# Four edits to the order of work: first weight pieces on one queue, splits ahead of casts, RG-LRU gates together, squares in another ring

## The chip, the core and the metric

The kernel runs on one core of one Trainium2 chip. The core has engines that run side by side, each in the order of its own queue: TensorE (PE; its weight loads are shown apart, as PEld), VectorE (DVE), ScalarE (ACT), GpSimd (POOL) and SyncE (SP). The metric is the device time of one execution in microseconds; lower is better. Before the change it is 1039.3 us, the median of three runs from 1038.3 to 1039.59.

## What is computed

A trunk of two layers over 256 tokens of width 2048, in float32. The even layer mixes tokens with an HGRN2 (8 heads of 128) beside a Griffin RG-LRU (8 blocks of 128); the odd layer with a chunkwise mLSTM (8 heads, keys of 128, values of 256). Each is followed by an output projection and a gated embedding. Cut to what the change touches:

```python
def rg_lru(xc, w_r, b_r, w_i, b_i, lam):           # even layer, 8 blocks of 128 features
    r  = sigmoid(einsum('bsnc,ncd->bsnd', xh, w_r) + b_r)
    ig = sigmoid(einsum('bsnc,ncd->bsnd', xh, w_i) + b_i)
    log_a = -8 * r * softplus(-lam)
    a = exp(log_a)
    u = sqrt(-expm1(2 * log_a)) * (ig * xf)
    h = scan(h -> a * h + u)

def mlstm(q, k, v, li, lf):                        # odd layer, per head
    sc  = einsum('bhtd,bhsd->bhts', q, k) * wts    # stabilised exponential weights
    num = (state part) + einsum('bhts,bhse->bhte', sc, v)

pl = rmsnorm(p[i] @ ple_w[i]) * ple_norm[i]        # embedding of width 256, at the very start for i = 0
h  = h + sigmoid(h @ ple_gate_w[i]) * pl
```

## The kernel before

**Products in three terms.** A float32 product is made from two rounded parts of each operand, high and low: high by high, high by low, low by high. For each weight piece `load_weights` (L121) issues a load into a `raw` tile (ring of 5), a cast to the high part `whi` on ScalarE (L132), and the subtraction that gives the low part `wlo` on VectorE (L133); `whi` and `wlo` have rings of 4 tiles of 128 x 1024. The three matmuls of a term group are L193, L194, L195. A projection of 512 columns is made in four quarters of the 2048 input features. A quarter has two tiles of weights and 24 matmuls: 12 for the first 128 tokens, 12 for the other 128, so that the first tile is done with after 18 of them. Results stand in PSUM: pool `pm` (tag `mm`, 3 tiles), `px` (tag `mx`, 3 tiles), `pst` (tag `st`, 2 tiles).

**Order of the work.** The code is written as a chain of projections on TensorE, with the rest of the layer in coroutines ("lanes"). In the middle of each quarter `pump` (L75) moves every lane one `yield` further, so TensorE's part of a lane is placed behind the matmul issued last. A planner orders each engine's queue by priority: an instruction's place in the program, less the offset of `tc.high_priority(offset=...)` around it. The weight casts and subtractions carry offset 400 (L131), the reading of the second branch's gate projection 450 (L876), some other readings of PSUM 100. Tiles of one tag share a ring of slots; a new tile waits for the last reader of the slot's old content.

**The start.** The first work is the embedding's projection. `load_head` (L268) loads the first two feature blocks of `p` and the first weight tile in four pieces of 256 columns each, through SP's queue (`sy`) and ScalarE's (`s`), and splits them at offset 900 (L280 to L286). `embed` (L289) runs the matmuls (L316): first those that need only the first half of the features, then those that need pieces three and four. Loads of everything after go through SP's queue in program order.

**RG-LRU** (`rg_lru`, L778), one coroutine for each half of the 8 blocks: split of inputs and weights; gates of blocks 0 and 1 (`j = 0`: matmuls L151 to L153 through `mm3`, sigmoids L801, in `st` tiles), a `yield`, gates of blocks 2 and 3, a `yield`; then tanh and exponential (L808, L809), squares (L814, in two tiles of tag `th`, a ring of 2) and L815, which reads them; square root; scan. The gate projection of the second branch (L873 to L886) reads its PSUM with a tanh into a tile of the same tag `th` (L879), a scaled copy (L880) and a product (L881). Tag `hn` is another ring, of 3 tiles, for scaled projections and rearranged features. The attention of the even layer (L610 on) uses `mx` tiles at the same stage.

**mLSTM.** Queries and keys come from a projection, a convolution (L979) and a SiLU (L982, L983). `mix(j)` (L1051) handles heads 2j and 2j+1: it spreads the running maxima (L231), builds the weights, splits queries and keys into high and low parts (L1074 on ScalarE, L1075 on VectorE), forms the scores (L1081, L1082), multiplies (L1083), splits again, and multiplies by the values (L1101). Meanwhile the values are projected in four groups (L1126): ScalarE writes the scaled high part `vt` from PSUM (L1133), VectorE the low part `vl` (L1134); both tiles of `pm` that a group holds come free with that.

Of the kernel before, what the change touches and what calls it, by code (L numbers as in the profile page):

```python
# [11 lines left out]
F32 = mybir.dt.float32  # L12
# [3 lines left out]
AF = mybir.ActivationFunctionType  # L16
ALU = mybir.AluOpType
PSUM = bass.MemoryType.PSUM

P = 128  # L20
# [23 lines left out]
def trunk(ctx: ExitStack, tc: tile.TileContext, a, out):  # L44
    nc = tc.nc
    v, s, gp, te, sy = nc.vector, nc.scalar, nc.gpsimd, nc.tensor, nc.sync
# [5 lines left out]
    tp = ctx.enter_context(tc.tile_pool(name="tp", bufs=2))  # L52
    bp = ctx.enter_context(tc.tile_pool(name="bp", bufs=4))
    pm = ctx.enter_context(tc.tile_pool(name="pm", bufs=3, space=PSUM))
    px = ctx.enter_context(tc.tile_pool(name="px", bufs=3, space=PSUM))
    pst = ctx.enter_context(tc.tile_pool(name="pst", bufs=2, space=PSUM))
# [211 lines left out]
    def load_head(src):  # L268
        praw = tp.tile([P, 512], F32, name="praw", tag="hn", bufs=3)
        raw = wp.tile([P, 1024], F32, name="raw", tag="raw", bufs=5)  # L270
        hi, lo = (wp.tile([P, 1024], F32R, name=n, tag=n) for n in ("whi", "wlo"))
        ph, pl, both = act_pair()

        def piece(x, n):
            return x[:, n * T:(n + 1) * T]

        for q, dst, of, n in ((sy, praw, a["pT"][0], 0), (s, raw, src, 0), (sy, praw, a["pT"][0], 1), (s, raw, src, 1),
                              (sy, raw, src, 2), (sy, raw, src, 3)):
            q.dma_start(out=piece(dst, n), in_=piece(of, n))
        with tc.high_priority(offset=900):  # L280
            for n in range(4):
                if n < 2:
                    v.tensor_copy(ph[:, n], piece(praw, n))
                    v.tensor_tensor(out=pl[:, n], in0=piece(praw, n), in1=ph[:, n].bitcast(F32), op=ALU.subtract)
                s.copy(piece(hi, n), piece(raw, n))
                v.tensor_tensor(out=piece(lo, n), in0=piece(raw, n), in1=piece(hi, n).bitcast(F32), op=ALU.subtract)  # L286
        return (hi, lo), (ph, pl, both)
# [175 lines left out]
    norm = {}  # L463
# [48 lines left out]
    def gate_tok(w, j, act, u):  # L512
# [7 lines left out]
    mx, e0, e1, lb, omb, sp, ez, z2, pol, sp8, spm8 = (small(8, n) for n in (  # L520
        "mx", "e0", "e1", "lb", "omb", "sp", "ez", "z2", "pol", "sp8", "spm8"))
# [44 lines left out]
    if True:  # L566
# [211 lines left out]
        def rg_lru(r):  # L778
            while r not in xcs:
                yield  # L780
            xc = xcs[r]
            bw = wp.tile([P, 2, 512], F32, name="bw", tag="raw", bufs=5)
            sy.dma_start(out=bw, in_=a["bw"][r])
            av = m0.tile([P, 1024], F32, name="av", tag="f")
            tt = m0.tile([P, 1024], F32, name="tt", tag="k")
            it = m0.tile([P, 1024], F32, name="it", tag="it", bufs=1)
            bh, bl = (hp.tile([P, 2, 512], F32R, name=n, tag="h") for n in ("bh", "bl"))
            s.copy(bh, bw)
            v.tensor_tensor(out=bl, in0=bw, in1=bh.bitcast(F32), op=ALU.subtract)
            xs = [split_act(xc[:, j * 512:(j + 1) * 512], "xc") for j in range(2)]  # L790
            yield
            for j in range(2):
                for w, (dst, bias) in enumerate(((av, "bbr"), (it, "bbi"))):
                    ps = pst.tile([P, 512], F32, name="st", tag="st")
                    for i in range(2):
                        c = 2 * j + i
                        mm3(ps[:, i * T:(i + 1) * T], bh[:, w, c * P:(c + 1) * P], bl[:, w, c * P:(c + 1) * P], xs[j], i,
                            True, True)
                    for i in range(2):
                        c = 2 * j + i  # L800
                        gate = s.activation(dst[:, c * T:(c + 1) * T], ps[:, i * T:(i + 1) * T], AF.Sigmoid,  # L801
                                            bias=pc(bias, 4 * r + c)).ins
                yield
            for c in range(4):
                b = 4 * r + c
                cc = slice(c * T, (c + 1) * T)
                with tc.issue_after(gate):
                    s.activation(tt[:, cc], av[:, cc], AF.Tanh, scale=sp8[:, b:b + 1])  # L808
                    s.activation(av[:, cc], av[:, cc], AF.Exp, scale=spm8[:, b:b + 1])  # L809
            v.tensor_tensor(out=it, in0=it, in1=xc, op=ALU.mult)  # L810
            for j in range(2):
                sq = tp.tile([P, 512], F32, name="sq", tag="th")
                jj = slice(j * 512, (j + 1) * 512)
                s.activation(sq, av[:, jj], AF.Square)  # L814
                v.scalar_tensor_tensor(tt[:, jj], sq, 1.0, tt[:, jj], op0=ALU.add, op1=ALU.mult)  # L815
            yield
            s.activation(tt, tt, AF.Sqrt, scale=0.25)
            v.tensor_tensor(out=it, in0=it, in1=tt, op=ALU.mult)
            yield
            v.memset(av.rearrange("p (c t) -> p c t", t=T)[:, :, 0:1], 0.0)  # L820
            v.tensor_tensor_scan(tt, av, it, 0.0, op0=ALU.mult, op1=ALU.add)
            res["h", r] = tt
# [50 lines left out]
        for g in range(2):  # L873
            ps = project_tok(ew, 6 + g, acth)
# [81 lines left out]
    with tc.tile_pool(name="m1", bufs=2) as m1:  # L956
        qk = {}
# [93 lines left out]
        def mix(j):  # L1051
# [17 lines left out]
                yield  # L1069
            qhl = room2("qhl").rearrange("p (s i t) -> p s i t", s=2, i=2)  # L1070
            khl = tp.tile([P, 512], F32R, name="khl", tag="th").rearrange("p (s i t) -> p s i t", s=2, i=2)
            for hl, src in ((qhl, qk[j].rearrange("p (i t) -> p i t", i=2)),
                            (khl, qk[4 + j].rearrange("p (i t) -> p i t", i=2)[:, :, 0:P])):
                s.copy(hl[:, 0], src)  # L1074
                v.tensor_tensor(out=hl[:, 1], in0=src, in1=hl[:, 0].bitcast(F32), op=ALU.subtract)  # L1075
            yield
            for i in range(2):
                q, k = qk[j][:, i * T:(i + 1) * T], qk[4 + j][:, i * T:(i + 1) * T]
# [13 lines left out]
            vh, vl = vts[j]  # L1092
# [33 lines left out]
        for j in range(4):  # L1126
            psv = project_tok(a["ov"], j, acth)
            vt = m1.tile([P, 2, 2, VW], F32R, name="vt", tag="vt", bufs=6)
            gp.memset(vt.bitcast(F32)[:, :, :, 256:VW], 1.0)
            vl = ap.tile([P, 1024], F32R, name="vl", tag="ahl").rearrange("p (h i e) -> p h i e", h=2, i=2)  # L1130
            for hf in range(2):
                src = psv[hf].rearrange("p (i e) -> p i e", i=2)
                s.activation(vt[:, hf, :, 0:256], src, AF.Copy, scale=norm["rt"][:, hf:hf + 1])  # L1133
                v.scalar_tensor_tensor(vl[:, hf], src, norm["rt"][:, hf:hf + 1], vt[:, hf, :, 0:256].bitcast(F32),  # L1134
                                       op0=ALU.mult, op1=ALU.subtract)
            vts.append((vt, vl))
            if j == 0:
                drain("qk0", "qk2")
                for c in range(4):
                    start("mix", mix(c))  # L1140
                start("mix", mix_norm())
# [259 lines left out]
```

## Time and profile before

| what | value |
|---|---|
| median of 3 runs | 1039.3 us (1038.3 to 1039.59) |
| profiled execution, its own time | 1037.71 us |
| its span, first to last instruction | 1035.9 us |
| granted TensorE clock | 0.998 |
| moved by DMA | 234.79 MB, mean 227 GB/s |
| VectorE, weight subtractions L133 | 357, 431.2 us together |
| ScalarE, weight casts L132 | 357, 372.7 us together |

How to read it: times within the execution are microseconds from the start of the span. In the list of waits a row is "who waited <- for whom", with the total, the number of times and the longest. In a timeline a row has the start, the duration, the engine, the line, the operation, the tile written <- the tiles read, the shapes and the count; brackets give the idle time before it and what ended it. Matmuls overlap, so a matmul's duration is longer than the distance to the next one's start.

### The profile page before, as it was taken

To read this page: it belongs to the slowest core of one execution; us is meant where nothing else is said; L and a number is where in the kernel's file an instruction comes from. 1 tells how busy PE (TensorE), PEld (TensorE's weight loads), DVE (VectorE), ACT (ScalarE), POOL (GpSimd) and SP (SyncE) were. 2 spreads that over 40 slices of the span, in tenths; PEclk is the share of its full clock that TensorE was granted. 3 is DMA by queue.
4 is the path that set the end of the run, shared out by engine and by line. 5 is a ranking of instruction groups with operands and counts; after the bars stand their busy time and mean duration, and the time that the engine had idled before them with its cause. 6 is when DMAs were issued, how large, how long until landed. Compare 5 with 4: busy or idle time off the path is not lost.

```text
span 1035.9 us, 14422 instructions
## 1 busy us (share of the span) xinstructions
PE 1025.0 (99%) x5230; PEld 851.1 (82%) x5230; DVE 739.9 (71%) x1130; ACT 599.6 (58%) x863; POOL 89.7 (9%) x169
## 2 busy tenths in 40 slices
PE   9999999999999999999999999999999999999996
PEld 7888888888888888888888888888888888888886
DVE  7858878969686776767569986755457777666684
ACT  7775555577874444565557865644445557344562
POOL 0111101011111121111021000000001111111000
PEclk9999999999999999999999999999999999999999
DMA  9987746567779888687597655455566778787552
GB/s 341 336 240 241 228 152 216 183 197 233 239 239 303 273 246 271 215 269 233 193 280 239 213 171 173 157 182 190 194 200 224 250 255 288 216 278 238 204 184 82
DMA packets 67752, 234.79 MB, mean 227 GB/s; under 512 B 8801, under 2 KB 10081, under 8 KB 67681
## 3 DMA queue, kind: packets, MB, share of 16 engines
q1 hardware_dynamic: 55728, 196.64, 57.5%
q0 software_dynamic: 11520, 36.71, 12.2%
q8 instruction: 41, 0.67, 0.3%
q10 hardware_dynamic: 432, 0.52, 0.2%
q14 instruction: 31, 0.25, 0.1%
HBM read 216.02 MB, written 17.83 MB: 226 GB/s over the span
## 4 chain that ended last, share of the span: by engine, by line
PE 96%; DVE 2%; ACT 1%; issue 1%; DMA 0%; SPq 0%; ACTq 0%; DVEq 0%
PE mm L193 26%; PE mm L195 26%; PE mm L194 26%; PE mx L195 4%; PE mx L193 4%; PE mx L194 3%; PE mm L316 2%; PE nu L1101 1%; DVE wlo L133 1%; PE mm L1233 1%; PE mm L1232 1%; PE mm L1231 1%; PE mx L626 0%; DVE qk L979 0%; DMA raw<-in_pw_dram 0%
## 5 line engine op out<-in xcount | busy, mean ns | idle before, releaser
L133 DVE TENSOR_TENSOR wlo<-raw,whi 128x1024 fp32r<-128x1024 f32 (+1 forms) x357 | 431.2, 1215 | 213.9 <-ACT whi L132 201.7
L132 ACT CAST whi<-raw 128x1024 fp32r<-128x1024 f32 (+1 forms) x357 | 372.7, 1048 | 315.7 <-PE mm L195 248.8
L193 PE MATMUL mm<-whi,ahl 128*128 128x512 f32 x1216 | 474.9, 391 | 0.1
L194 PE MATMUL mm<-wlo,ahl 128*128 128x512 f32 x1216 | 473.4, 389 | 0.0
L195 PE MATMUL mm<-whi,ahl 128*128 128x512 f32 x1216 | 473.0, 389 | 0.0
L193 PEld LDWEIGHTS mm<-whi,ahl 128*128 128x128 f32 x1216 | 228.3, 188 | 48.4 <-issue 0.8
L195 PEld LDWEIGHTS mm<-whi,ahl 128*128 128x128 f32 x1216 | 228.3, 188 | 47.9
L194 PEld LDWEIGHTS mm<-wlo,ahl 128*128 128x128 f32 x1216 | 228.3, 188 | 46.9 <-DVE wlo L133 0.3
L193 PE MATMUL mx<-whi,ahl 128*128 128x512 f32 x160 | 62.2, 389 | 0.0
L194 PE MATMUL mx<-wlo,ahl 128*128 128x512 f32 x160 | 62.2, 389 | 0.0
L195 PE MATMUL mx<-whi,ahl 128*128 128x512 f32 x160 | 62.2, 389 | 0.0
L194 PEld LDWEIGHTS mx<-wlo,ahl 128*128 128x128 f32 x160 | 30.0, 188 | 6.3
L195 PEld LDWEIGHTS mx<-whi,ahl 128*128 128x128 f32 x160 | 30.0, 188 | 6.2
L193 PEld LDWEIGHTS mx<-whi,ahl 128*128 128x128 f32 x160 | 30.1, 188 | 6.2
L477 POOL DMA_DIRECT2D ducn<-w x4 | 2.2, 559 | 214.4 <-DVE w L490 214.4
L979 DVE SCALAR_TENSOR_TENSOR qk<-xr,prm,qk 128x255 f32<-128x255 f32 (+2 forms) x48 | 20.5, 471 | 0.1
L147 DVE TENSOR_TENSOR ahl<-xr,ahl 128x512 fp32r<-128x512 f32 x24 | 16.3, 686 | 4.1 <-ACT ahl L146 4.0
L316 PE MATMUL mm<-whi,ahl 128*128 128x512 f32 x56 | 17.4, 389 | 0.0
L146 ACT CAST ahl<-xr 128x512 fp32r<-128x512 f32 x24 | 14.7, 612 | 4.2 <-DVE xr L831 4.1
L361 DVE STREAM_TRANSPOSE w<-hq 128x512 f32<-128x512 f32 x24 | 16.7, 703 | 0.2
L379 DVE TENSOR_TENSOR ahl<-r,ahl 128x128 fp32r<-128x128 f32 x64 | 13.9, 280 | 2.8 <-ACT ahl L377 2.8
L377 ACT CAST ahl<-r 128x256 fp32r<-128x256 f32 x32 | 10.6, 402 | 5.7 <-DMA r<-dfe 5.6
(330 smaller groups left out, 824.4 us busy)
## 6 DMA issues: line engine op xcount, KB each, us to landing
raw<-in_ew_dram SPq DMA_DIRECT2D x64, 512.0 KB, 5.5
raw<-in_g_dram SPq DMA_DIRECT2D x64, 512.0 KB, 5.1
raw<-in_eo_dram SPq DMA_DIRECT2D x32, 512.0 KB, 5.9
raw<-in_oqk_dram SPq DMA_DIRECT2D x32, 512.0 KB, 4.8
raw<-in_ov_dram SPq DMA_DIRECT2D x32, 512.0 KB, 4.1
raw<-in_oog_dram SPq DMA_DIRECT2D x32, 512.0 KB, 3.7
raw<-in_oz_dram SPq DMA_DIRECT2D x32, 512.0 KB, 4.2
raw<-in_oo_dram SPq DMA_DIRECT2D x32, 512.0 KB, 5.2
```

Of the source, the lines that this page charges most:

```text
L132: last["act"] = s.copy(h, r).ins
L133: last["dve"] = v.tensor_tensor(out=l, in0=r, in1=h.bitcast(F32), op=ALU.subtract).ins
L146: (v.tensor_copy if name == "p0" else s.copy)(hi, src)
L147: v.tensor_tensor(out=lo, in0=src, in1=hi.bitcast(F32), op=ALU.subtract)
L193: te.matmul(ps[hf], xh, wh, start=(k == 0), stop=False)
L194: te.matmul(ps[hf], xh, wl, start=False, stop=False)
L195: last["pe"] = te.matmul(ps[hf], xl, wh, start=False, stop=(k == KT - 1)).ins
L316: last["pe"] = te.matmul(ps[hf][:, o:o + w_], tokens(pact[x], k, hf), (hi, lo)[y][:, k * 512 + o:k * 512 + o + w_], start=(n == mine[0]), ...
L361: v.transpose(w5[:, hf], h[:, hf].rearrange("p (c j q) -> p c j q", c=4, j=4))
L377: s.copy(hk, src)
L379: v.tensor_tensor(out=lk[:, hf], in0=src[:, hf], in1=hk[:, hf].bitcast(F32), op=ALU.subtract)
L979: v.scalar_tensor_tensor(dst[:, sh:T], pi[:, 0:T - sh], pc("ccw", k * 16 + n), dst[:, sh:T], op0=ALU.mult, op1=ALU.add)
```

## The change

Four edits. (1) In `load_head` pieces three and four of the first weight tile are issued on ScalarE's queue, as pieces one and two are. (2) In `rg_lru` the gates of both pairs of blocks are computed in one step of the coroutine, the second pair in `mx` tiles, and two `yield`s follow. (3) The squares take tiles of the ring `hn` instead of `th`. (4) The splits of queries and keys, and the reading of the values from PSUM with their split, carry offset 450.

```diff
         for q, dst, of, n in ((sy, praw, a["pT"][0], 0), (s, raw, src, 0), (sy, praw, a["pT"][0], 1), (s, raw, src, 1),
-                              (sy, raw, src, 2), (sy, raw, src, 3)):
+                              (s, raw, src, 2), (s, raw, src, 3)):
             q.dma_start(out=piece(dst, n), in_=piece(of, n))
...
             for j in range(2):
                 for w, (dst, bias) in enumerate(((av, "bbr"), (it, "bbi"))):
-                    ps = pst.tile([P, 512], F32, name="st", tag="st")
+                    pool, tag = ((pst, "st"), (px, "mx"))[j]
+                    ps = pool.tile([P, 512], F32, name="rg", tag=tag)
...
-                yield
+            yield
+            yield
             for c in range(4):
...
-                sq = tp.tile([P, 512], F32, name="sq", tag="th")
+                sq = tp.tile([P, 512], F32, name="sq", tag="hn", bufs=3)
...
-            for hl, src in ((qhl, qk[j].rearrange("p (i t) -> p i t", i=2)),
-                            (khl, qk[4 + j].rearrange("p (i t) -> p i t", i=2)[:, :, 0:P])):
-                s.copy(hl[:, 0], src)
-                v.tensor_tensor(out=hl[:, 1], in0=src, in1=hl[:, 0].bitcast(F32), op=ALU.subtract)
+            with tc.high_priority(offset=450):
+                for hl, src in ((qhl, qk[j].rearrange("p (i t) -> p i t", i=2)),
+                                (khl, qk[4 + j].rearrange("p (i t) -> p i t", i=2)[:, :, 0:P])):
+                    s.copy(hl[:, 0], src)
+                    v.tensor_tensor(out=hl[:, 1], in0=src, in1=hl[:, 0].bitcast(F32), op=ALU.subtract)
...
-            for hf in range(2):
-                src = psv[hf].rearrange("p (i e) -> p i e", i=2)
-                s.activation(vt[:, hf, :, 0:256], src, AF.Copy, scale=norm["rt"][:, hf:hf + 1])
-                v.scalar_tensor_tensor(vl[:, hf], src, norm["rt"][:, hf:hf + 1], vt[:, hf, :, 0:256].bitcast(F32),
-                                       op0=ALU.mult, op1=ALU.subtract)
+            with tc.high_priority(offset=450):
+                for hf in range(2):
+                    src = psv[hf].rearrange("p (i e) -> p i e", i=2)
+                    s.activation(vt[:, hf, :, 0:256], src, AF.Copy, scale=norm["rt"][:, hf:hf + 1])
+                    v.scalar_tensor_tensor(vl[:, hf], src, norm["rt"][:, hf:hf + 1], vt[:, hf, :, 0:256].bitcast(F32),
+                                           op0=ALU.mult, op1=ALU.subtract)
```

## The prediction

> **What bounds the kernel now.** I read the page first, then the list of who waited for whom, cut down to TensorE and its weight loads, and then the timeline at the few places which that list names.
>
> ```profile
> span 1035.9 us, 14422 instructions
> ...
> PE 1025.0 (99%) x5230; PEld 851.1 (82%) x5230; DVE 739.9 (71%) x1130; ACT 599.6 (58%) x863; POOL 89.7 (9%) x169
> ```
>
> TensorE is busy for 1025.0 of 1035.9 us. The edits remove no matmul, so they can only win back time in which TensorE stands still. The waits of TensorE and of its weight loads:
>
> ```profile
> PE mx L316 <- ACT whi L285: 1.1, 1, 1.1
> ...
> PE mx L1081 <- DVE khl L1075: 0.5, 1, 0.5
> ...
> PEld mm L193 <- ACT u L880: 0.4, 1, 0.4
> ...
> PEld mm L193 <- PE mx L231: 0.3, 1, 0.3
> ```
>
> Columns: who waited, for whom, us in total, times, longest. There are four short places: the start (L316), the score products (L1081), and two places where a projection (L193) cannot start on its next PSUM tile. Each edit touches one of them. These rows count idle time from the modelled end of a matmul, so below I size each place by the distance between matmul starts.
>
> **Part 1, the first weight pieces (L277).** The chain of waits and ScalarE's timeline in the first microseconds:
>
> ```profile
> 2.12 4.40 DMA raw<-in_pw_dram
> 6.55 0.41 ACT whi L285
> ...
> 7.00 2.11 PE mx L316 x8
> ```
>
> ```profile
> 0.74 0.89 ACTq L279 DMA_DIRECT2D raw<-in_pw_dram  x2
> 1.66 1.28 ACT L285 ACT_TABLE_LOAD   x1 [1.66 <-PEq L1392]
> 3.90 0.40 ACT L285 CAST whi<-raw 128x256 fp32r<-128x256 f32 x1 [0.95 <-DMA raw<-in_pw_dram]
> ...
> 7.60 1.27 ACT L132 CAST whi<-raw 128x512 fp32r<-128x512 f32 x2 [0.65 <-DMA raw<-in_pw_dram]
> ```
>
> The fourth piece is issued on SP at 2.12, lands 4.40 us later and is cast at 6.55; only then can the products with the second half of the features begin (7.00). The edit puts pieces three and four behind the first two on ScalarE's queue. Two issues there take 0.89 us, so the third starts at about 0.74 + 0.89 = 1.63 and the fourth at 2.08: the same moment as now. Nothing is won at the issue itself. ScalarE pays two more issues, 0.89 us, and its table load slides from 1.66 to about 2.55, ending at 3.83: still before the first piece is cast at 3.90, so it is covered, with 0.07 us to spare. SP is free 0.9 us sooner, and all its later loads go out that much earlier: the second half's pieces, the next block, the parameters, the first activations.
>
> So the question is when the fourth piece lands once it no longer stands in SP's line. The first 10 us of the transfers (issues with median us to landing; GB/s in 40 slices of 0.25 us):
>
> ```profile
> GB/s 1 0 0 0 0 0 0 135 205 246 213 279 373 369 373 279 238 205 209 148 188 238 246 270 246 279 270 295 270 279 295 311 295 311 336 360 377 303 367 308
> ...
> raw<-in_pw_dram SPq DMA_DIRECT2D x4, 256.0 KB, 5.2
> ...
> raw<-in_pw_dram ACTq DMA_DIRECT2D x2, 128.0 KB, 3.2
> ```
>
> Best end: it lands as fast as ScalarE's pieces do now, 3.2 us after issue, at 5.3; the wait of 1.1 us goes. Worst end: it shares the engines with SP's 256 KB pieces, which are now issued at 1.66 and 2.12, and takes their 5.2 us: 7.3, which is 0.8 us later than now. Bytes say something between: from 1.75 to 6.5 us the slices average about 249 GB/s, 1.18 MB, and the six first pieces with two 256 KB ones are 1.31 MB, which would be done by about 7.0. So -1.1 to +0.8; I take 0, since the row nearest to it is the piece itself, issued at the same moment with 4.40.
>
> [...]
>
> [...]
>
> ```profile
> 580.23 1.05 ACT L132 CAST whi<-raw 128x1024 fp32r<-128x1024 f32 x1 [0.78 <-PE mm L195]
> 581.30 1.28 ACT L982 ACT_TABLE_LOAD   x1
> 582.59 0.63 ACT L982 ACTIVATE th<-qk 128x512 f32<-128x512 f32 x1
> ```
>
> The cast ends at 581.28, the load runs from 581.30 to 582.58 and the next activation starts at 582.59. I go by these rows.
>
> **Part 2, RG-LRU: gates in one group, squares in another ring (L792 to L815).** The same 24 x 2 gate matmuls and 16 sigmoids run; those of the second pair of blocks move up by one step of the coroutine, and two `yield`s keep the exponentials where they were. Their PSUM comes from the three `mx` tiles. The attention uses these too, but one at a time until its read-out, a step later; I cost this at nothing, and if the cover were gone it is a wait of one evacuation, the 0.69 us of the row at 282.26 below. The gain lies at the first gate projection of the second branch. TensorE and ScalarE there:
>
> ```profile
> 282.97 0.39 PE L195 MATMUL mm<-whi,ahl 128*128 128x512 f32 x1
> 283.20 0.88 PE L193 MATMUL mm<-whi,ahl 128*128 128x512 f32 x2
> 283.92 0.39 PE L194 MATMUL mm<-wlo,ahl 128*128 128x512 f32 x1
> ```
>
> ```profile
> 270.41 0.84 ACT L801 ACTIVATE av<-st,prm 128x256 f32<-128x256 f32 x2 [1.74 <-PE st L153]
> ...
> 282.26 0.69 ACT L879 ACTIVATE th<-mm,rth 128x512 f32<-128x512 f32 x1 [0.84 <-DVE tt L815]
> 282.85 0.68 ACT L880 ACTIVATE u<-mm,rcr 128x512 f32<-128x512 f32 x1
> ```
>
> The columns are start, duration and, in brackets, the idle time before. A matmul normally follows the last by 0.23 us (282.97 to 283.20). From 283.20 two of them take 0.72 us to the next start instead of 0.46: 0.26 us lost, because the PSUM tile is only free once L880 has read it at 283.53. L880 is late because the tanh before it stood idle 0.84 us for L815: its `th` slot was still held by a square. With the squares in `hn` that wait goes and L880 ends about 0.8 us earlier, before 283.20. The gates moved away from 270.41 free another 2 x 0.84 us of ScalarE ahead of it. **Gain 0.26 us**; bounds 0 and 0.26.
>
> **Part 3, values split ahead of the casts (L1131).** TensorE, ScalarE and VectorE at the first group of values:
>
> ```profile
> 589.55 0.39 PE L231 MATMUL mx<-s,identr 128*128 128x256 f32 x2
> 590.04 0.47 PE L193 MATMUL mm<-whi,ahl 128*128 128x512 f32 x1
> 590.35 0.39 PE L194 MATMUL mm<-wlo,ahl 128*128 128x512 f32 x1
> ```
>
> ```profile
> 584.63 0.69 ACT L1133 ACTIVATE vt<-mm,rcr 128x512 fp32r<-128x512 f32 x1
> ...
> 588.03 0.68 ACT L1133 ACTIVATE vt<-mm,rcr 128x512 fp32r<-128x512 f32 x1
> ```
>
> ```profile
> 589.14 0.75 DVE L1134 SCALAR_TENSOR_TENSOR vl<-mm,rcr,vt 128x512 fp32r<-128x512 f32 x1
> ```
>
> ScalarE has read the first half by 585.32, but VectorE reads it last only from 589.14 to 589.89; the next projection's second tile is the same bank, and it starts at 590.04. Two 256-column matmuls and the restart take 0.80 us from 589.55 to 590.35 instead of about 0.46: 0.34 us lost. Moved ahead of the weight casts, the subtraction follows ScalarE by the time VectorE is next free, more than 3 us early. **Gain 0.34 us**; bounds 0 and 0.34.
>
> **Part 4, queries and keys split ahead of the casts (L1074).** The first and the second head pair on TensorE, then VectorE and ScalarE at the first:
>
> ```profile
> 606.48 0.52 PE L1081 MATMUL mx<-qhl,khl 128*128 128x256 f32 x3
> ...
> 608.36 0.47 PE L193 MATMUL mm<-whi,ahl 128*128 128x512 f32 x1
> ```
>
> ```profile
> 627.23 0.52 PE L1081 MATMUL mx<-qhl,khl 128*128 128x256 f32 x3
> ...
> 628.30 0.48 PE L193 MATMUL mm<-whi,ahl 128*128 128x512 f32 x1
> ```
>
> ```profile
> 603.85 0.69 DVE L983 SCALAR_TENSOR_TENSOR qk<-th,qk 128x512 f32<-128x512 f32 x1 [0.76 <-ACT th L982]
> 604.79 2.36 DVE L133 TENSOR_TENSOR wlo<-raw,whi 128x1024 fp32r<-128x1024 f32 x2 [0.25 <-ACT whi L132]
> 607.07 0.42 DVE L1075 TENSOR_TENSOR khl<-qk,khl 128x256 fp32r<-128x256 f32 x1
> ```
>
> ```profile
> 605.61 0.40 ACT L1074 CAST khl<-qk 128x256 fp32r<-128x256 f32 x1
> ```
>
> The group takes 1.88 us to the next projection at the first pair and 1.07 at the second: 0.81 us lost. The keys are ready at 604.54, but their split waits for two weight casts on ScalarE and then for 2.36 us of weight subtractions. Put ahead, it needs 0.40 + 0.42 us and is done by about 606.0 even behind one subtraction; TensorE asks for it near 606.8. What is pushed back is two weight pieces, by 0.8 us at most. **Gain 0.81 us**; bounds 0 and 0.81.
>
> **The sum.** 0 + 0.26 + 0.34 + 0.81 = 1.41 us. The profiled execution took 1037.71 us, 1.81 outside its span; less 1.41 it is 1036.3. The median of the three runs shown, 1039.3, stands 1.59 above the profiled one, so on that scale the forecast is **1037.9 us**, 0.14% below before. A measurement of this kernel can tell about 0.2%, 2.1 us, from no change.
>
> **Rivals.**
>
> *Early piece.* The fourth piece lands at 5.3 and TensorE's 1.1 us go too. For it: the 3.2 us of ScalarE's pieces. Against it: the next casts themselves wait for data at 7.60, which caps the gain at some 0.7 us unless the 256 KB pieces also come sooner; being issued 0.9 us earlier, they may. 1.41 + 1.1 = 2.5: 1036.8.
>
> *Late piece.* +0.8 at the start: gain 0.6, 1038.7. [...]
>
> *Blocked casts, the slower side.* ScalarE works in order. If the planner puts the reading of the value tiles ahead of weight casts that could have run earlier, these stand behind a wait for TensorE. At the first group: the second half of the values is read at 588.03, to 588.71. If the pair of casts from 580.23 on stood behind it, the first would be cast and subtracted by 588.71 + 1.05 + 1.18 (half of the 2.36) = 590.94. There are four such tiles; a cast starts when one comes free and is used 30 matmuls, 6.8 us, later, so the first low-part use of this one is here:
>
> ```profile
> 587.05 0.39 PE L194 MATMUL mm<-wlo,ahl 128*128 128x512 f32 x1
> ```
>
> That is 3.9 us of standstill; less the 0.26 and 0.81 that stay, +2.8: 1042.1. It decides as soon as a cast is held past 584.8 (587.05 less 2.23), where now it starts at 580.23. For it: L879 and L880 already have this same priority, and casts do come behind them. Against it: TensorE lost only 0.26 us there, by a ring.
>
> *No new order.* The planner leaves the queues as they are: 1039.3.
>
> **How the numbers follow.** Forecast 0.48 (its own range 1037.0 to 1038.7: the start 0.9 better or 0.8 worse); early piece 0.20; late piece 0.08; blocked casts 0.20, since every piece moved in front delays casts that feed the engine which sets the end; no new order 0.04. Faster by over 0.2% needs 2.1 us: 0.13 of the forecast's chance, where the start wins 0.7, and 0.19 of the early piece's: 0.32. Slower by over 0.2%: 0.19 of the blocked casts and 0.01 of the late piece: 0.20. Within: 0.48. The range runs from 1036.3, the early piece with half a microsecond for the scatter of runs, to 1041.6, into the blocked casts.
>
> **What would show it.** Right: no wait of TensorE on `khl`, on `u` of L880, or after L231; L1134 right behind L1133; khl's subtraction ahead of the pair of `wlo`; L879 without a wait on L815; the table load near 2.55 and the first cast still near 3.9. The start of the second L316 group tells the early piece (5.8 to 6.3), no change (7.0) and the late one (7.8) apart. Wrong: a wait of TensorE on `whi` or `wlo` after 200 us, or on an `mx` tile near 208 or 215, and every gain above with a new standstill of equal size behind it.

## The result, and the profile after

The change made the kernel slower by a hair: 1040.51 us median of 14 runs (1038.28 to 1041.98) against 1038.17 us for the kernel before (14 runs, 1037.73 to 1040.18). The ratio is 1.0017 with an interval of 1.0010 to 1.0024. The forecast was 0.14% faster; it is 0.17% slower. The three runs of before that were shown at first (1039.3) lay above what that kernel mostly does: in four series, 110 runs in all, its median is from 1038.2 to 1038.6. Of the executions below one, the profiled one of the change without its first edit (e9), was disturbed (1141.38 us at a granted clock of 0.85) and is left out.

The profiled execution of after, at 1038.36 us, is one of its two shortest. Two rows of its page:

```profile
span 1036.5 us, 14418 instructions
...
PE 1024.9 (99%) x5230; PEld 851.5 (82%) x5230; DVE 740.1 (71%) x1130; ACT 600.2 (58%) x863; POOL 89.7 (9%) x169
```

The same matmuls, the same busy time, and the span 0.6 us longer than the 1035.9 of before. So the difference is again in TensorE's waits. The list of waits of TensorE in after, whole:

```profile
PE mx L316 <- ACT whi L285: 1.7, 1, 1.7
PE st L97 <- PEq L1396: 0.8, 1, 0.8
PE mm L194 <- DVE wlo L133: 0.7, 1, 0.7
```

The reader sees three things beside the list of before. The wait for the keys' split (`khl`, 0.5) is gone. The wait at the start has grown from 1.1 to 1.7. And there is a new one, on `wlo`, the low part of a weight piece.

**The start.** The chain of waits of after in the first microseconds, and ScalarE's timeline there:

```profile
2.14 5.57 DMA raw<-in_pw_dram
7.73 0.41 ACT whi L285
...
8.18 2.10 PE mx L316 x8
```

```profile
0.74 1.85 ACTq L279 DMA_DIRECT2D raw<-in_pw_dram  x4
2.62 1.28 ACT L285 ACT_TABLE_LOAD   x1 [2.62 <-issue]
3.92 0.40 ACT L285 CAST whi<-raw 128x256 fp32r<-128x256 f32 x1
```

The fourth piece is issued at 2.14, as before, but lands 5.57 us later in place of 4.40. The products that need it begin at 8.18 in place of 7.00. The issue list of the first 10 us has the load on both queues:

```profile
raw<-in_pw_dram SPq DMA_DIRECT2D x4, 256.0 KB, 4.7
...
raw<-in_pw_dram ACTq DMA_DIRECT2D x4, 128.0 KB, 4.3
```

ScalarE's pieces took 3.2 us when there were two of them and take 4.3 now that there are four; SP's large pieces gained, from 5.2 to 4.7.

**The RG-LRU.** ScalarE and TensorE of after at the first gate projection of the second branch (two lines were added above, so `th` is L881, `u` L882, the square root L819):

```profile
278.68 0.67 ACT L881 ACTIVATE th<-mm,rth 128x512 f32<-128x512 f32 x1
...
280.88 1.28 ACT L819 ACT_TABLE_LOAD   x1
...
283.26 1.28 ACT L881 ACT_TABLE_LOAD   x1
284.55 0.69 ACT L881 ACTIVATE th<-mm,rth 128x512 f32<-128x512 f32 x1
...
285.71 2.94 ACT L132 CAST whi<-raw 128x1024 fp32r<-128x1024 f32 x3
```

```profile
286.82 0.72 PE L193 MATMUL mm<-whi,ahl 128*128 128x512 f32 x2
287.38 0.39 PE L194 MATMUL mm<-wlo,ahl 128*128 128x512 f32 x1
288.45 0.50 PE L194 MATMUL mm<-wlo,ahl 128*128 128x512 f32 x1 [0.68 <-DVE wlo L133]
288.79 0.39 PE L195 MATMUL mm<-whi,ahl 128*128 128x512 f32 x1
```

Before, both readings came ahead of the table load; its rows for the second reading and the load are:

```profile
283.42 0.69 ACT L879 ACTIVATE th<-mm,rth 128x512 f32<-128x512 f32 x1
...
284.70 1.28 ACT L817 ACT_TABLE_LOAD   x1
```

The stop at 283.20 is gone, and so is the tanh's wait for L815: `th` now begins at 278.68. But the square root, with the table load ahead of it and the one behind it, has slipped in between the reading of the first tile (from 278.68) and that of the second (from 284.55). From 280.88 to 284.54 ScalarE does nothing but this, and three weight casts stand behind the late reading, from 285.71. TensorE comes for them: 287.38 to 288.45 is 1.07 us where 0.23 is normal (0.84 lost), and 286.82 to 287.38 and 288.45 to 288.79 lose 0.10 and 0.11. That is 1.05 us against the 0.26 saved.

**The splits.** TensorE in after at the first pair of heads (scores are L1084 now):

```profile
607.85 0.52 PE L1084 MATMUL mx<-qhl,khl 128*128 128x256 f32 x3
...
608.93 0.48 PE L193 MATMUL mm<-whi,ahl 128*128 128x512 f32 x1
```

They take 1.08 us to the next projection, where they took 1.88. The stop at 590 behind L231 is gone too: no wait of TensorE's weight loads on L231 is left in after. Nothing has come in the place of either.

So the profiled executions add up. The first product of the attention, L626, before and after:

```profile
96.29 0.89 PE L626 MATMUL mx<-q,k 128*32 128x48 f32 x64
```

```profile
97.25 0.89 PE L626 MATMUL mx<-q,k 128*32 128x48 f32 x64
```

It runs 0.96 us later. +0.96 at the start, +0.79 (1.05 less 0.26) in the RG-LRU, -0.34 and -0.81 at the splits make +0.6, as the spans have it. But the medians differ by 2.3 us, so most executions of after lose something more that this one did not. That took experiments.

### The profile page after: what moved, and what is told of

Read it like the earlier page. It is cut to its first block, busy times and chain, and to the rows that moved or that the text cites. A ratio compares the mean times of both kernels' runs of the same rounds, so it can differ in the third digit from the quotient of the medians.

```text
span 1036.5 us, 14418 instructions
## 1 busy us (share of the span) xinstructions
PE 1024.9 (99%) x5230; PEld 851.5 (82%) x5230; DVE 740.1 (71%) x1130; ACT 600.2 (58%) x863; POOL 89.7 (9%) x169
## 4 chain that ended last, share of the span: by engine, by line
PE 96%; ACT 2%; issue 1%; DMA 1%; DVE 0%; ACTq 0%; DVEq 0%
PE mm L193 26%; PE mm L194 26%; PE mm L195 26%; PE mx L194 4%; PE mx L193 4%; PE mx L195 3%; PE mm L316 2%; PE nu L1104 1%; PE mm L1236 1%; PE mm L1237 1%; PE mm L1235 1%; DMA raw<-in_pw_dram 1%; PE mx L626 0%; ACT whi L132 0%; PE mx L747 0%
## 5 line engine op out<-in xcount | busy, mean ns | idle before, releaser
L316 PE MATMUL mm<-whi,ahl 128*128 128x512 f32 x56 | 17.4, 389 | 0.0
L517 ACT ACTIVATE u<-mm,rth 128x512 f32<-128x512 f32 x12 | 8.2, 683 | 7.6 <-PE mm L195 7.6
```

Source lines behind the costliest of these rows:

```text
L316: last["pe"] = te.matmul(ps[hf][:, o:o + w_], tokens(pact[x], k, hf), (hi, lo)[y][:, k * 512 + o:k * 512 + o + w_], start=(n == mine[0]), ...
```

## The experiments

They are called e1 to e12; the name stands with each result. All are timed beside runs of the kernel before; its median was 1038.43 (35 runs) in the series of the first four, 1038.46 (33) in that of the second four and 1038.63 (28) in that of the last four.

### The four edits, each alone

The first part of the change alone:

```diff
-                              (sy, raw, src, 2), (sy, raw, src, 3)):
+                              (s, raw, src, 2), (s, raw, src, 3)):
```

> Before, with the first edit alone (pieces three and four on ScalarE's queue). Theory: the fourth piece shares the DMA engines with SP's 256 KB pieces and lands at about 7.7 us instead of 6.5, TensorE's first wait grows from 1.1 to about 1.7 us and everything after it starts about 1 us later; and since the changed kernel's own runs mostly take 1 to 3 us longer than its profiled one, this start also costs more in most runs than in that profile: median 1.5 to 3 us slower than before, with a wide scatter. Rival (the start costs the 1 us of the profile and no more, the scatter comes from elsewhere): 0.7 to 1.2 us slower, scatter as before. Rival from the prediction (no change at the start): within 0.4 us.

Measured (e1): 1040.63 us (12 runs, 1038.37 to 1043.23), ratio 1.0020 (1.0012 to 1.0029). This one edit, which I had put at nothing, is as large as the whole loss. Its profiled execution was the longest of the twelve, and it shows what the profile of after doesn't. From its chain of waits, and then its busy time and granted clock (PEclk) in two stretches:

```profile
7.61 3.41 PE mx L316 x8
```

```profile
core 0: us, PE busy (x) PEld busy (x) DVE busy (x) ACT busy (x) POOL busy (x), PEclk, DMA share, GB/s
...
3.61:7.02 3.41, 1.99 (x13) 1.41 (x11) 2.44 (x7) 1.51 (x4) 0.00 (x0) 1.00 0.98 346
7.04:10.43 3.39, 2.82 (x7) 2.25 (x8) 2.74 (x5) 2.49 (x5) 0.00 (x0) 0.50 1.02 365
```

The eight products behind the wait take 3.41 us here and 2.11 in the chain of before, 1.30 more, since the granted clock is at one half from 7.04 to 10.43. In the stretch just before it TensorE was busy for only 1.99 of 3.41 us, because it waited 1.65 us for the piece. The half-clock stretch lasts about 3.41 us, and it costs 1.30 us here.

Not all that this execution lost is at the start. Its list of waits has a second one:

```profile
PE mx L194 <- DVE wlo L133: 1.8, 1, 1.8
```

It lies at 871 us: the loads of `row`, for which VectorE waited 2.6 us in before, kept it 7.7 us here, and a weight subtraction stood behind. Behind this wait, too, the clock is granted at half, from 874.0 to 877.4 us. No other profile has this wait, so I do not count it to the edit. The run's mean clock, 0.995, fits two such stretches and the half-clock end (below).

The fourth part alone, the splits of queries, keys and values (two places):

```diff
+            with tc.high_priority(offset=450):
```

> Before, with the fourth edit alone (splits of queries, keys and values at offset 450). Theory: the waits at 589.7 and 606.7 us go and nothing takes their place: 1.1 us faster (0.34 + 0.81), 0.11%. Rival (blocked casts: the values' reading holds weight casts up): 0 to 3 us slower, with a wait of TensorE on whi or wlo between 585 and 670 us.

Measured (e2): 1037.2 us (11 runs, 1036.32 to 1038.03), ratio 0.9987 (0.9978 to 0.9995), 1.23 us below before. Its profiled execution has neither the wait on `khl` nor the late projection at 590. The two terms summed to 1.15.

The second part alone, the gates in one group:

```diff
-                    ps = pst.tile([P, 512], F32, name="st", tag="st")
+                    pool, tag = ((pst, "st"), (px, "mx"))[j]
+                    ps = pool.tile([P, 512], F32, name="rg", tag=tag)
...
-                yield
+            yield
+            yield
```

> Before, with the second edit alone (RG-LRU gates in one group). Theory: grouping the gates pulls the exponentials and the square root of the second half forward, so that the square root's and the tanh's table loads stand ahead of the second reading of the gate projection and of three weight casts; TensorE then waits about 1 us for wlo near 286 us: 0.6 to 1.0 us slower than before. Rival (the moved squares do that, not the gates): 0 to 0.3 us faster, no wait of TensorE near 286 us.

Measured (e3): 1039.45 us (11 runs, 1038.84 to 1040.91), ratio 1.0009 (1.0001 to 1.0018), 1.02 us above before. From its waits of TensorE:

```profile
PE mm L194 <- DVE wlo L133: 0.7, 1, 0.7
...
PE mm L193 <- ACT whi L132: 0.3, 1, 0.3
```

The new stop of after is here, alone, and a little larger: both waits lie between 286.4 and 288.8 us, and by the distances of matmul starts they lose 0.41 and 0.84.

The third part alone, the squares:

```diff
-                sq = tp.tile([P, 512], F32, name="sq", tag="th")
+                sq = tp.tile([P, 512], F32, name="sq", tag="hn", bufs=3)
```

> Before, with the third edit alone (squares in the ring hn). Theory: the tanh at 282.3 us no longer waits for the squares' reader and TensorE's 0.26 us near 283 us go: 0.2 to 0.4 us faster. Rival (the squares' ring is what reorders ScalarE's queue): 0.6 to 1.0 us slower, with TensorE's wait for wlo near 286 us.

Measured (e4): 1038.29 us (11 runs, 1037.43 to 1039.33), ratio 0.9997 (0.9988 to 1.0005): no difference that can be told. In its profile the reading no longer waits for L815. The second of the two readings and the square root's table load there:

```profile
282.16 0.68 ACT L880 ACTIVATE u<-mm,rcr 128x512 f32<-128x512 f32 x1
...
286.73 1.28 ACT L817 ACT_TABLE_LOAD   x1
```

With this edit alone the load keeps its place behind both readings.

The four medians together: +2.20 - 1.23 + 1.02 - 0.14 = +1.85 us, where the whole change has +2.34 by the medians and +1.8 by the ratio. The parts add up within their intervals.

### Why the late piece costs 2 us and not 1

The first edit again, with four throw-away matmuls behind the first eight products, so that TensorE has work while it waits:

```diff
+                    if head and c == 0 and n == 7:
+                        for _ in range(4):
+                            with tc.issue_after(last["pe"]):
+                                last["pe"] = te.matmul(busy[:, 0:P], fill, fill, start=True, stop=True).ins
```

> The first edit (the fourth weight piece on ScalarE's queue) with four more throw-away 128 by 128 matmuls on TensorE behind the first eight products, where it otherwise stands idle for 1.66 us until the fourth piece is cast. Theory (the later piece costs about 1 us by itself, and in many executions another 1.4 us because a whole 3.41 us stretch of the granted clock then comes out at half speed): the piece lands as late as in the first edit alone (5.5 to 5.9 us of chain), so the time stays about 1 us above before, but no stretch after 6.5 us is at half clock; median 1039.3 (1038.8 to 1039.9), its runs within 1.5 us of each other, the granted clock of nearly every run 0.997 or more. Rival (the half-clock stretch has nothing to do with TensorE's idle time): median 1040.6 and a scatter of some 4 us as in the first edit alone, with clocks of 0.994 to 0.997. Rival (the throw-away matmuls run on past the landing and hold up the real ones): first product after the wait later than 8.3 us and a median above 1040.6.

Measured (e5): 1039.06 us (11 runs, 1038.52 to 1039.5), ratio 1.0005 (0.9997 to 1.0014). In its profiled execution the piece was even later than in after; TensorE (the four throw-away matmuls, L322, stand as eight entries) and ScalarE:

```profile
6.19 1.05 PE L322 MATMUL st<-const-float32-1.0 128*128 128x128 f32 x8
8.48 1.19 PE L316 MATMUL mx<-whi,ahl 128*128 128x512 f32 x4 [1.23 <-ACT whi L285]
```

```profile
8.02 0.40 ACT L285 CAST whi<-raw 128x256 fp32r<-128x256 f32 x1 [0.63 <-DMA raw<-in_pw_dram]
```

The first product after the wait begins at 8.48, 0.87 later than in the first edit's own profile, and yet the median is 1.57 us lower, since the four products run at full speed (1.19 us; the same four took 2.08 in e1). The mean granted clock of each run, which is read without a trace, tells it for all of them:

| kernel | clock 0.997 or 0.998: runs, median us | clock 0.994 to 0.996: runs, median us |
|---|---|---|
| before (three series) | 86, 1038.43 | 10, 1039.57 |
| the whole change | 2, 1038.32 | 12, 1040.57 |
| first edit alone | 2, 1039.19 | 10, 1040.87 |
| first edit, wait filled | 11, 1039.06 | none |

One stretch of 3.41 us at half clock lowers the mean over 1037 us by 0.5 x 3.41 / 1037 = 0.0016. Each profiled execution also ends at half clock, for its last 3.3 to 6.3 us, and that alone gives 0.998 or 0.997. So, as an estimate from these profiles for the runs without a trace, a run at 0.996 or less has one such stretch or more, a run at 0.998 has none, and 0.997 can be either (the profile of e12, below, has one and a mean of 0.997). The kernel before has it in one run of ten, the first edit in ten of twelve; with the wait filled no run is below 0.997, and nine of the eleven are at 0.998. So of the 2.2 us of this edit about 0.6 are the later piece itself (1039.06 - 1038.46) and about 1.6 go with the half-clock stretches, most of them the one that follows the longer wait. Where in a run without a trace the stretch lay can't be seen; that it goes when TensorE's wait is filled is what ties it to the wait.

### What makes the piece late

On SP's queue the fourth piece went ahead of the 256 KB transfers; on ScalarE's it runs beside them. My assumption, to be tested, was that the two queues take turns; then smaller transfers on SP's queue should let it through sooner and larger ones later, at the same number of bytes. Both, each with the first edit (four of 128 KB, then one of 512 KB, in place of two of 256 KB):

```diff
-                parts = [part] + load_weights(w[0], (1, 2), (1,))
+                parts = [part] + load_weights(w[0], (1, 4), (1,))
```

> The first edit, and the second half of the first weight tile, which SyncE's queue moves beside it, in four transfers of 128 KB in place of two of 256 KB. Theory (the fourth piece is late because its packets take turns with those of the larger transfers on the other queue): the size of the transfer it shares with hardly alters the turns, but each turn of the other queue is shorter; the fourth piece's chain is 4.8 to 5.3 us in place of 5.57, TensorE's first wait 1.0 to 1.4 us in place of 1.7 to 1.9, and the median 0.4 to 1.2 us below the first edit alone (1039.4 to 1040.2). Rival (the turns go by bytes, whatever the size of the transfers): landing at 5.5 to 5.9 us, first wait 1.6 to 1.9 us, median 1040.3 to 1041, plus what two more issues on SyncE cost.

```diff
-                parts = [part] + load_weights(w[0], (1, 2), (1,))
+                parts = [part] + load_weights(w[0], (1, 1), (1,))
```

> The first edit, and the second half of the first weight tile, which SyncE's queue moves beside it, in one transfer of 512 KB in place of two of 256 KB. Theory (the fourth piece's packets take turns with those of the transfer on the other queue, and a turn of a larger transfer is longer): the fourth piece is cast later than in the first edit alone, at 8.0 to 9.0 us in place of 7.2 to 7.8, TensorE waits 1.9 to 3 us there, and the median is 0.5 us or more above the first edit alone (1041.1 or more). Rival (only the number of bytes ahead counts, which is the same): cast at 7.2 to 7.8 us, median 1040.2 to 1041.

Measured, small (e6): 1039.42 us (11 runs, 1038.74 to 1040.08), ratio 1.0010 (1.0001 to 1.0018). Large (e12): 1041.88 us (6 runs, 1041.29 to 1042.69), ratio 1.0030 (1.0019 to 1.0042). The cast of the fourth piece on ScalarE, small and then large:

```profile
6.87 0.40 ACT L285 CAST whi<-raw 128x256 fp32r<-128x256 f32 x1 [0.30 <-DMA raw<-in_pw_dram]
```

```profile
8.90 0.41 ACT L285 CAST whi<-raw 128x256 fp32r<-128x256 f32 x1 [0.57 <-DMA raw<-in_pw_dram]
```

The same bytes stand on the other queue, but one profile for a size is little against a scatter of 0.9 us among the three with 256 KB, and four small issues, by my estimate, take SP longer than two large ones (its five issues in a row from 1.65 us took 3.52 us in after), so that the bytes may also come later. The lists of transfers of the five profiles show how the two queues shared the time. This is what each queue moved from 2 to 5 us, while the fourth piece was still under way in all of them:

| profile, transfers beside the piece | SP's queue: packets, MB | ScalarE's queue: packets, MB | fourth piece cast at, us |
|---|---|---|---|
| e6, 128 KB | 474, 0.43 | 461, 0.42 | 6.87 |
| e1, 256 KB | 379, 0.47 | 385, 0.36 | 7.16 |
| after, 256 KB | 392, 0.49 | 372, 0.35 | 7.73 |
| e5, 256 KB | 342, 0.40 | 344, 0.32 | 8.02 |
| e12, 512 KB | 306, 0.43 | 294, 0.27 | 8.90 |

In each of the five, both queues move the same number of packets, within 6%. A packet on ScalarE's queue is some 0.9 KB in all of them; on SP's the mean grows from 0.9 KB (e6) to 1.4 KB (e12) with the transfers. So here, the larger the transfers, the fewer bytes of the pieces got through in the same time (0.42 MB in e6, 0.27 in e12), and the later the last one was cast. Equal counts fit the assumption of turns, but in what order the packets went is not shown; nor is why e5 moved fewer of them (686) than e1 and after (764 each) at equal sizes.

The small one has its price. Its first wait is 0.72 us, less than before's 1.06 and than the 1.0 to 1.4 expected, and still its median is 0.96 above before. In its waits there is another:

```profile
PE mx L316 <- ACT whi L285: 0.7, 1, 0.7
...
PE mm L316 <- ACT pl L328: 0.3, 1, 0.3
```

```profile
12.24 1.05 ACT L132 CAST whi<-raw 128x1024 fp32r<-128x1024 f32 x1 [1.09 <-DMA raw<-in_pw_dram]
```

The next tile of weights now lands late, its cast keeps ScalarE waiting 1.09 us, and the reading of PSUM behind it (L328) comes late for TensorE. Another 0.3 us lies outside the span: its runs took 2.06 to 2.24 us more than their spans, where those of the other kernels took 1.72 to 1.90. Why is not shown.

### Whether it is the square root's place

The second edit, with one more turn of the planner's order between the squares and the square root:

```diff
             yield
+            yield
             s.activation(tt, tt, AF.Sqrt, scale=0.25)
```

> The second edit (the gates in one group) with one more turn of the planner's order between the squares and the square root, so that ScalarE makes both readings th, u of the next weight tile ahead of the first table load, as it did before the change. Theory (the second edit costs time because the square root and its two table loads slip ahead of a reading, whose weight casts then come late at 286 us): the waits at 286.5 and 287.7 us (0.41 and 0.84 us) are gone, and the median is 0.7 to 1.2 us below the second edit alone: 1038.1 to 1038.7, with a ratio to before of 0.9995 to 1.0003. Rival (it is the other ring for the gates' sums that costs): the median stays at 1039.2 to 1039.7 and TensorE still waits about 1.2 us between 280 and 290 us.

Measured (e7): 1038.1 us (11 runs, 1037.28 to 1039.33), ratio 0.9998 (0.9989 to 1.0007): 1.35 us below the second edit alone, level with before. ScalarE there, from the second reading on (`th` L882, square root L820):

```profile
280.68 0.70 ACT L882 ACTIVATE th<-mm,rth 128x512 f32<-128x512 f32 x1
...
281.83 1.06 ACT L132 CAST whi<-raw 128x1024 fp32r<-128x1024 f32 x1
282.91 1.28 ACT L820 ACT_TABLE_LOAD   x1
```

The second reading comes 3.9 us earlier than in after (280.68 for 284.55), a weight cast follows it ahead of the table load, and TensorE has no wait at all between 255 and 310 us. The `mx` tiles for the gates' sums are still there, so they cost nothing; it was the place of the square root.

### The parts together, without the first

The third and fourth parts:

> The third and fourth edits alone: squares in the other ring, splits of queries, keys and values ahead of the weight casts; the first weight pieces and the gates as before. Theory (the parts add up): the waits at 589.7 us (0.34) and 606.7 us (0.81) are gone, and the one at 283 us (0.27) too; median 1.2 to 1.5 us below before, 1036.7 to 1037.3, ratio 0.9984 to 0.999. Rival (the squares' ring moves something else, as it did the gates' order): a median at or above that of the splits alone, 1037.2 or more, with a new wait of 0.2 us or more between 260 and 310 us.

Measured (e8): 1036.96 us (11 runs, 1036.22 to 1038.11), ratio 0.9985 (0.9976 to 0.9994).

The whole change without its first edit:

> The whole change but for its first edit: the fourth weight piece stays on SyncE's queue. Theory (the parts add up: gates +1.0, squares and splits -1.5, head +2.2 us, each measured alone): median 0.3 to 0.8 us below before, 1037.7 to 1038.2, and 2.0 to 2.8 us below the whole change. Rival (the parts act on one another, the planner's order of one undoing the stall of another): outside 1037.4 to 1038.6.

Measured (e9): 1037.85 us (10 runs, 1037.41 to 1038.82), ratio 0.9991 (0.9982 to 1.0000), 2.7 us below the whole change. The parts add up once more.

The same with the square root one turn later, as in the run above:

> The gates in one group with the one more turn of the planner's order ahead of the square root, the squares in the other ring and the splits ahead of the weight casts; the fourth weight piece as before. Theory (every stall between 260 and 310 us and those of 589.7 and 606.7 us are gone, and only the head's wait is left): median 1.4 to 1.9 us below before, 1036.5 to 1037.1; no wait of 0.15 us or more of TensorE between 260 and 310 us. Rival (the gates' grouping, with its stall mended, is worth nothing beyond the squares' 0.27 us, which ends the same stall): equal to squares and splits alone within 0.2 us, 1036.8 to 1037.2. Rival (a new order of the planner late in the kernel): 1037.5 or more.

Measured (e10): 1036.89 us (11 runs, 1036.4 to 1038.14), ratio 0.9984 (0.9975 to 0.9993). It is 0.07 from splits and squares alone, so the mended grouping of the gates is worth nothing beyond the squares; the two cannot be told apart. Its profiled execution has by chance what the rival "early piece" wished for. ScalarE in it:

```profile
5.82 0.41 ACT L285 CAST whi<-raw 128x256 fp32r<-128x256 f32 x1 [0.23 <-DMA raw<-in_pw_dram]
...
11.91 1.05 ACT L132 CAST whi<-raw 128x1024 fp32r<-128x1024 f32 x1 [1.21 <-DMA raw<-in_pw_dram]
```

and its waits of TensorE:

```profile
PE mm L316 <- ACT pl L328: 1.0, 1, 1.0
```

The fourth piece is cast at 5.82 and TensorE doesn't wait for it, but it pays 1.02 us at 12.5, since the next tile lands at 11.88: the wait only moved. In this execution the start is held by its loads as a whole, not by this piece.

The last one fills the wait of the unchanged start with the four throw-away matmuls:

> The same as e10_late_splits_squares, with four throw-away 128 by 128 matmuls on TensorE in the wait of the head (1.1 us, from 5.7 to 6.9 us). Theory (a stretch of the granted clock that falls mostly into TensorE's wait makes the next 3.41 us run at half speed in some executions): no run with a granted clock below 0.997, all runs within 1.3 us of each other, and a median 0 to 0.4 us below e10. Rival (the throw-away matmuls run past the landing, since the clock is still half at 5.7 us): first product after the wait 0.1 to 0.6 us later than 7.0 us, and the median as much above e10.

Measured (e11): 1036.8 us (11 runs, 1036.15 to 1038.01), ratio 0.9981 (0.9972 to 0.9990). No run is below a clock of 0.997, as expected, but the runs are 1.86 us apart, not 1.3, and the median is e10's within 0.1: with the short wait of before only one run in ten had a half-clock stretch to lose. By the ratios this and e10 are 0.16 to 0.19% below before; by the medians, from different series, they are some 0.35% below the whole change.

## Why the prediction was wrong, point by point

**What bounds the kernel** was read rightly: every difference found inside the span is TensorE standing still, or running at half clock in the 3.41 us that followed a wait (of 1.65 us in e1, 1.11 us in e8). Reading only the idle time missed the second.

**Part 1 is the first step that failed, and it failed twice.** "I take 0, since the row nearest to it is the piece itself, issued at the same moment with 4.40": the 4.40 us held for a piece that stood ahead of the large transfers in SP's line. Moved to the other queue it runs beside them, and landed after 4.99 to 5.86 us in the three profiles with this start (e1, after, e5). The start of the second L316 group, which was to tell the cases apart, came at 8.18, beyond the 7.8 of "late piece". The worst end, +0.8, was about right for that (0.96 in the profiled pair, 0.6 by e5). What the sum did not have at all is the granted clock: with the longer wait a stretch at half speed comes in most runs (ten of twelve in e1, by their mean clocks), and with it some 1.6 us more of the median (1040.63 less the 1039.06 of e5). The rest of the part came as worked out: the fourth piece is issued at 2.14 (2.08 expected), the table load is at 2.62 (2.55), the first cast at 3.92 (3.9). No time is lost behind the load, as in the rows at 581 us of before: the load ends at 3.90 and the cast begins at 3.92.

**Part 2**: the squares' term was right as a mechanism. With the squares in `hn` the wait on L815 and the stop at 283.20 go (e4; the grouping alone, e3, ends that wait too), and 0.26 us is too little for the median to show. The bounds of 0 and 0.26 were wrong, since they left no room for a loss. This is the second step that failed: I argued that "two `yield`s keep the exponentials where they were", and looked no further. They did not keep even those (the table load ahead of them moved from 273.72 to 271.89), and the square root behind them moved from 284.70 to 280.88, and there it splits the two readings of PSUM with two table loads. e7 shows it: one more turn for the square root, and the 1.0 us is gone. The wait on an `mx` tile, which I did name as a risk, never came.

**Parts 3 and 4** were right in place and size: 1.15 forecast, 1.23 measured alone, both stops gone and no new one behind them. The casts that were pushed back had time.

**The rivals.** "Late piece" was the true one for the start; I gave it 0.08, though the bytes I had counted myself (done by about 7.0) spoke for it, and priced it without the clock. "Blocked casts" did not come where I had put it, at the values, but its mechanism did, at the square root. "Early piece", at 0.20, was worth nothing in the one execution that had it, e10's profiled one.

**The sum.** 0 + 0.26 + 0.34 + 0.81 was to be a gain of 1.41. The median it started from, 1039.3, was itself about 1 us above what more runs gave. Measured alone, part by part: -2.20 at the start, -0.88 for gates and squares, +1.23 for the splits, a loss of 1.85.

## What to carry to other kernels

A small transfer that an engine waits for was best left ahead of the large ones in their own queue here; on the other queue it ran beside them, both queues moving as many packets within 6%, and landed after 4.99 to 5.86 us in place of 4.40. When an operation is moved earlier, follow all that stands behind it in its engine's queue up to the next table load (1.28 us each here), not only the operation itself. And price a TensorE wait with the clock that it may cost behind it: here 3.41 us at half speed after waits of 1.11 us (e8) and 1.65 us (e1), none after one of 1.66 us (after). Some throw-away matmuls in the wait are a cheap test of that; in e5 they took 1.57 us off the median.

## What the runs showed of the hardware that I had not expected

After a wait of 1.11 us the granted clock was at one half for about 3.41 us in one execution; after one of 1.66 us it stayed full in another. In e8, which has before's start, TensorE waited 1.11 us and the four products behind the wait took 2.08 us; in after it waited 1.66 us and they ran at full speed:

```profile
7.06 2.08 PE L316 MATMUL mx<-whi,ahl 128*128 128x512 f32 x4 [1.11 <-ACT whi L285]
```

```profile
8.18 1.19 PE L316 MATMUL mx<-whi,ahl 128*128 128x512 f32 x4 [1.66 <-ACT whi L285]
```

Each trace holds the list of clock grants, which places the stretches. It begins with the first full grant, at 3.6 to 6.8 us of the span, another time in each execution (PEclk counts what comes ahead of it as full), and in before and after the drop to half at the end comes a whole number of 3.413 us later (1027.41 us, 301 times, and 1024.00 us, 300 times). Until that first grant TensorE runs slower as well: in before products of 256 columns start 0.21 us apart up to the grant at 5.17, and 0.12 to 0.13 apart from then on. Counted in stretches of 3.41 us from the first grant: in e1, e4 and e8 the first full stretch began at 3.6 to 3.9, held nearly all of the wait, and the next stretch was at half; so it was in e12 (5.41, with a wait of 2.42). TensorE was busy for 1.0 to 2.0 us of that stretch in these four. In before and seven of the runs it was busy for 2.3 us or more, and the clock stayed full. After is the exception: its first full stretch began at 6.45 and held the wait whole, with 1.75 us of work, and the next stayed full. So at the start, in these profiles, half stretches came only behind a first full stretch with 2.0 us of work or less, and the length of the wait tells less (1.11 us in e8, 1.66 us in after). By after, with 1.75 us of work, that is not the whole of it; what exactly is counted is not shown.

The landing of the same first transfers differs by about 1 us between executions of one and the same start (its fourth piece is cast from 7.16 to 8.02 with all pieces on ScalarE's queue, from 5.82 to 6.90 with before's start), as much as the largest of the gains that the change was made of.
